# Sample attention in one round per half of the samples instead of one per key head

## The chip, the cores and the metric

The kernel runs on one core of one Trainium2 chip. The metric is the time of one execution on the device, in microseconds, as the median of several runs. The core has a matrix engine (TensorE, "PE" in the profile; its loads of the stationary operand are "PEld"), a vector engine (VectorE, "DVE"), an activation engine (ScalarE, "ACT"), a general engine (GpSimd, "POOL"), and queues that issue DMAs, here mostly that of SyncE ("SP"). Products land in PSUM banks of 128 partitions x 512 floats; everything else lives in SBUF.

## The reference, cut to what matters

One layer of a hybrid decoder runs for a prompt of 1024 tokens and for 8 sample sequences of 8 new tokens each: a SwiGLU block, a mixing block (sliding-window attention beside a gated linear recurrence, "hgrn"), and a second SwiGLU block, all float32. The change concerns the attention of the samples, which see a cache of 128 older keys and values:

```python
def cached_window_attention(q, k, v, sinks, k_buf, v_buf):
    kk = jnp.concatenate([k_buf, k], axis=1)          # 128 cached + 8 new keys
    vv = jnp.concatenate([v_buf, v], axis=1)
    s = jnp.einsum('bqhgd,bkhd->bhgqk', q, kk) * SCALE # 2 key heads x 4 query heads, 64 wide
    dist = (Wb + jnp.arange(Ld))[:, None] - jnp.arange(Wb + Ld)[None, :]
    mask = (dist >= 0) & (dist <= WINDOW)
    p = sink_probs(s, mask, sinks)                     # softmax with a learned sink per head
    out = jnp.einsum('bhgqk,bkhd->bqhgd', p, vv)
```

## The kernel before

**Groups.** The tokens are worked on in three groups n = 0, 1, 2: 256 prompt tokens with the 64 sample tokens (width 320), and twice 384 prompt tokens. Dense products (`mm3`, lines 242 to 244: three products of split operands in place of one float32 product) make up nearly all of TensorE's work. They use four PSUM banks with the tag `mm`. All the small products of attention, recurrence, norms and transposes share four banks with the tag `ax` (`axbank`).

**Side work by steps.** The small work is written as generators that stop at each `yield`. Between pieces of dense work the kernel calls `tick()`, which advances two queues, `at` (attention) and `hg` (recurrence), and the streams of norms (`c0`, `c1`, `c2`, `half`), each with its rate. A queue entry carries a declared number of steps; `pace` divides the steps left by the ticks left until the group is due:

```python
DUE = {0: 132, 1: 208, 2: 256}
for n, _, left in q:
    sofar += left
    rate = max(rate, sofar / max(1, DUE[n] - now[0]))
owed[k] += rate        # whole steps that are owed are taken at this tick
```

Ticks are counted from the start of `w_in_units(0)`. That makes 44 ticks (the attention's entries of group 0 join the queue after 12 of them, the recurrence's after 36), then come the rest of the first SwiGLU's down products (`f1.pair`, 48 ticks), then `w_in_units(1)` (44), and at tick 136 `need_mix(0)` takes whatever steps of group 0 are left before `w_out_units(0)` uses the result. A prompt block (`attn_block`, declared 9 steps) really has 11 stops: scores and softmax of half its heads, transposes, value products, the same for the other half, then scaling, gain (`finish_attn`, L1137), transposes (L1142) and the split copy `put_mix` (L1128, L1129). The recurrence's sample part (`sample_hgrn`) runs in the other queue at the same time; its products write the tiles `skT`, `sav` and `su`. Streams `c1` and `c2` form the input of groups 1 and 2 (`post_n`, then `pre_n` with transposes at L419 and split copies at L423 and L424). L220 is the vector half of splitting weights, L949 empties the banks of `f1.pair`.

**Order on an engine.** Each engine takes its instructions in the order in which a scheduler lays them out when the kernel is built, from simulated times; `issue_after(x)` only fixes that an instruction stands behind x on its engine. Buffers are slots behind a tag: `t2` has eight slots, which the sample attention shares with the norms and the recurrence.

**The sample attention** (`sample_attn`) handles the samples in two halves `hb` of four, and in each half the two key heads `g` one after the other. A round for one `hb` and one `g` has three steps: scores (L1383: four products, one per sample, each of 64 rows and 32 columns, rows 0 to 63 for g = 0 and 64 to 127 for g = 1, into the tile `ssc`) with the softmax on VectorE and ScalarE; transposes of the probabilities (L1400, L1401, tile `spT`) with two copies; value products with the cached values (L1408) and with the 8 new ones (L1412), tile `spv`, then scaling and a DMA to `osc`. A float32 product appears as two records in the trace. Four rounds make 12 steps; with the loads ahead and the gathering and `finish_attn` behind there are 17.

Of the kernel before, what the change touches and what calls it, by code (L numbers as in the profile page):

```python
# [18 lines left out]
P = 128  # L19
# [25 lines left out]
def tile_step(ctx: ExitStack, tc: tile.TileContext, A: dict, O: dict):  # L45
# [17 lines left out]
    def axbank(s="ax"):  # L63
        return ps.tile([P, 512], F32, tag="ax", bufs=4, name=uid(s))
# [948 lines left out]
    def mixing(tp, h):  # L1013
# [339 lines left out]
        def sample_attn():  # L1353
# [23 lines left out]
            osc = dr.tile([4, P, 64], F32, name="osc")  # L1377
            for hb in range(2):
                vc = cached("cache_v_win", hb)
                for g in range(2):  # L1380
                    bank = axbank("ssc")
                    for i in range(4):
                        PE.matmul(bank[32 * i:32 * i + 32, :136],  # L1383
                                  qs[64 * g:64 * g + 64, 4 * hb + i].rearrange("p m t -> p (m t)"),
                                  keys[64 * g:64 * g + 64, 4 * hb + i], start=True, stop=True)
# [12 lines left out]
                    yield  # L1398
                    bank = axbank("spT")
                    PE.transpose(bank[:, :P], p[:, :P], ident)  # L1400
                    PE.transpose(bank[:8, P:2 * P], p[:, P:136], ident)  # L1401
                    pT = t2((P, 2, P))
                    V.tensor_copy(pT[:, 0], bank[:, :P])
                    V.tensor_copy(pT[:8, 1], bank[:8, P:2 * P])
                    yield
                    ob = axbank("spv")
                    for i in range(4):
                        PE.matmul(ob[32 * i:32 * i + 32, :64], pT[:, 0, 32 * i:32 * i + 32],  # L1408
                                  vc[:, i, g * 64:g * 64 + 64], start=True, stop=False, skip_group_check=True)
                    for i in range(4):  # L1410
                        c = i * P + g * 64
                        PE.matmul(ob[32 * i:32 * i + 32, :64], pT[:8, 1, 32 * i:32 * i + 32],  # L1412
                                  vnb[hb][:8, c:c + 64], start=False, stop=True, skip_group_check=True)
# [362 lines left out]
```

## Time and profile before

| what | value |
|---|---|
| median of 3 runs | 1960.67 us (1960.13 to 1961.73) |
| the profiled execution, its own time | 1958.28 us |
| its span in the profile | 1956.2 us |
| TensorE busy | 1942.2 us, 99% |
| VectorE busy | 1368.3 us, 70% |
| ScalarE busy | 930.1 us, 48% |
| granted TensorE clock | 0.999 |
| first and last start of the sample scores (L1383) | 841.1 and 903.3 us |

The span is the stretch from the first to the last instruction in the profile. A view by lines gives for each group of instructions its engine, the shape, the count, the busy time and the mean of one. A timeline gives start, duration and the instruction, with neighbours of one kind merged ("x8"). Matmuls are pipelined, so their durations overlap; the distance between the starts of two dense products is what one of them costs.

### The profile page before, as it was taken

To read this page: it belongs to the slowest core of one execution; us is meant where nothing else is said; L and a number is where in the kernel's file an instruction comes from. 1 tells how busy PE (TensorE), PEld (TensorE's weight loads), DVE (VectorE), ACT (ScalarE), POOL (GpSimd) and SP (SyncE) were. 2 spreads that over 40 slices of the span, in tenths; PEclk is the share of its full clock that TensorE was granted. 3 is DMA by queue.
4 is the path that set the end of the run, shared out by engine and by line. 5 is a ranking of instruction groups with operands and counts; after the bars stand their busy time and mean duration, and the time that the engine had idled before them with its cause. 6 is when DMAs were issued, how large, how long until landed. Compare 5 with 4: busy or idle time off the path is not lost.

```text
span 1956.2 us, 34187 instructions
## 1 busy us (share of the span) xinstructions
PE 1942.2 (99%) x13469; PEld 1826.3 (93%) x13469; DVE 1368.3 (70%) x2210; ACT 930.1 (48%) x1628; POOL 208.1 (11%) x213
## 2 busy tenths in 40 slices
PE   9999999999999999999999999999999999999998
PEld 8999999999998988788899998999999999999887
DVE  7976667876557666876677676755987877655666
ACT  6533333444445544644345565655544444444453
POOL 0000000000004112111232224011000000000202
PEclk9999999999999999999999999999999999999999
DMA  7443345556667546765434344556555645667874
GB/s 267 147 145 145 149 163 176 176 189 212 237 227 229 178 130 182 233 200 148 125 115 150 97 126 120 167 160 207 165 206 191 218 171 187 210 237 234 305 260 141
DMA packets 160396, 358.20 MB, mean 183 GB/s; under 512 B 16284, under 2 KB 59996, under 8 KB 160220
## 3 DMA queue, kind: packets, MB, share of 16 engines
q1 hardware_dynamic: 159228, 354.19, 54.9%
q8 instruction: 105, 1.72, 0.4%
q10 hardware_dynamic: 1008, 1.84, 0.3%
q14 instruction: 55, 0.45, 0.1%
HBM read 279.33 MB, written 77.63 MB: 182 GB/s over the span
## 4 chain that ended last, share of the span: by engine, by line
PE 95%; DMA 2%; DVE 2%; ACT 1%; issue 0%; POOL 0%; SPq 0%; DVEq 0%; POOLq 0%; ACTq 0%
PE mm L242 28%; PE mm L244 28%; PE mm L243 28%; DMA ar<-fa 1%; PE c L244 1%; PE c L242 1%; PE c L243 1%; PE sc L1163 1%; PE pv L1204 1%; PE lv L1237 1%; PE pT L1189 1%; DVE w L220 0%; PE av L1338 0%; PE su L1460 0%; PE av L1341 0%
## 5 line engine op out<-in xcount | busy, mean ns | idle before, releaser
L242 PE MATMUL mm<-h,wsph 128*128 128x320 f32 (+1 forms) x1296 | 415.6, 321 | 2.6 <-DVE sg L668 2.6
L243 PE MATMUL mm<-h,wsph 128*128 128x320 f32 (+1 forms) x1296 | 410.0, 317 | 0.0
L244 PE MATMUL mm<-h,wspl 128*128 128x320 f32 (+1 forms) x1296 | 408.3, 316 | 0.1
L220 DVE TENSOR_TENSOR wspl<-raw,wsph 128x1024 fp32r<-128x1024 f32 x200 | 250.3, 1252 | 148.3 <-ACT wsph L219 143.0
L219 ACT CAST wsph<-raw 128x1024 fp32r<-128x1024 f32 x200 | 209.1, 1048 | 298.1 <-PE mm L243 246.6
L219 ACT CAST w<-raw 128x512 fp32r<-128x512 f32 (+1 forms) x226 | 169.5, 754 | 242.0 <-PE mm L243 116.7
L220 DVE TENSOR_TENSOR w<-raw,w 128x512 fp32r<-128x512 f32 (+1 forms) x226 | 196.6, 873 | 85.0 <-ACT w L219 84.7
L242 PEld LDWEIGHTS mm<-h,wsph 128*128 128x128 f32 x1296 | 243.3, 188 | 9.7 <-issue 4.5
L243 PEld LDWEIGHTS mm<-h,wsph 128*128 128x128 f32 x1296 | 243.5, 188 | 1.8 <-issue 0.8
L244 PEld LDWEIGHTS mm<-h,wspl 128*128 128x128 f32 x1296 | 243.0, 188 | 1.9 <-issue 1.0
L242 PE MATMUL mm<-h,w 128*128 128x384 f32 x704 | 235.6, 335 | 0.0
L243 PE MATMUL mm<-h,w 128*128 128x384 f32 x704 | 235.6, 335 | 0.0
L244 PE MATMUL mm<-h,w 128*128 128x384 f32 x704 | 230.5, 335 | 0.0
L242 PE MATMUL mm<-w,h 128*128 128x512 f32 x462 | 181.5, 396 | 1.3 <-DVE big L949 1.3
L243 PE MATMUL mm<-w,h 128*128 128x512 f32 x462 | 180.2, 390 | 0.0
L244 PE MATMUL mm<-w,h 128*128 128x512 f32 x462 | 178.9, 391 | 0.3 <-DVE h L220 0.3
L213 POOL TENSOR_TENSOR sm<-sm,mhalf 128x3 f32<-128x3 f32 (+4 forms) x37 | 35.4, 960 | 1188.8 <-DVE sm L297 522.4
L242 PEld LDWEIGHTS mm<-h,w 128*128 128x128 f32 x704 | 132.1, 188 | 0.2 <-ACT big L763 0.2
L243 PEld LDWEIGHTS mm<-h,w 128*128 128x128 f32 x704 | 132.1, 188 | 0.0
L244 PEld LDWEIGHTS mm<-h,w 128*128 128x128 f32 x704 | 131.7, 188 | 0.0
L219 ACT CAST w<-t 128x512 fp32r<-128x512 f32 x176 | 106.9, 621 | 49.3 <-PE mm L244 46.0
L220 DVE TENSOR_TENSOR w<-t,w 128x512 fp32r<-128x512 f32 x176 | 118.6, 685 | 11.9 <-ACT w L219 11.8
(340 smaller groups left out, 3685.8 us busy)
## 6 DMA issues: line engine op xcount, KB each, us to landing
raw<-in_ffn_w_gu_dram SPq DMA_DIRECT2D x154, 512.0 KB
raw<-in_ffn_w_down_dram SPq DMA_DIRECT2D x74, 512.0 KB
raw<-in_w_in_dram SPq DMA_DIRECT2D x54, 512.0 KB
ar<-fa SPq DMA_DIRECT2D x70, 384.0 KB
big<-in_ffn_w_down_dram SPq DMA_DIRECT2D x88, 256.0 KB
fb<-big SPq DMA_DIRECT2D x44, 512.0 KB
raw<-fb SPq DMA_DIRECT2D x40, 512.0 KB
fa<-big SPq DMA_DIRECT2D x22, 768.0 KB
```

The costliest lines, as they stand in the source:

```text
L213: G.tensor_tensor(y, x, mhalf[:y.shape[0], :y.shape[1]], op=ALU.pow)
L219: S.copy(hi, src)
L220: return (lo_eng or V).tensor_tensor(lo, src, hi.bitcast(F32), op=ALU.subtract)
L242: PE.matmul(out, a[0], b[0], start=first, stop=False, skip_group_check=resume)
L243: PE.matmul(out, a[0], b[1], start=False, stop=False, skip_group_check=resume)
L244: return PE.matmul(out, a[1], b[0], start=False, stop=last, skip_group_check=resume)
L1163: PE.matmul(banks[g][:, i * 256:i * 256 + wk], zq[64 * g:64 * g + 64, 2 * pr + i, b * P:(b + 1) * P], kx[64 * g:64 * g + 64, k0:k0 + wk], ...
L1189: PE.transpose(bank[:, (i * nk + kb) * P:(i * nk + kb + 1) * P], pt[g][:, i, kb * P:(kb + 1) * P], ident)
L1204: PE.matmul(ob[q0:q0 + 64, c:c + 64], pT[g][:, k1:k1 + 64], vn[:, vb, g * 64:g * 64 + 64], start=kb == 0, stop=kb == nk - 1)
L1237: PE.matmul(b4[ps_, j, a], x[:, a, cs], y[:, a, cs], start=True, stop=True)
```

## The change

Both key heads of a half go through one round. The scores of g = 1 and then of g = 0 are issued into two banks (the second four held behind the first by `issue_after`), then the softmax is made for both; both pairs of transposes go into one bank, which two longer copies empty; the value products of both go side by side into one bank, head 0's cached and new values and then head 1's; two scalings and two DMAs follow. The round has three steps instead of twice three, and the entry in the queue declares 11 steps instead of 17.

```diff
             for hb in range(2):
                 vc = cached("cache_v_win", hb)
+                banks = [axbank("ssc") for _ in range(2)]
+                for g in (1, 0):
+                    with tc.issue_after(last) if g == 0 else nullcontext():
+                        for i in range(4):
+                            last = PE.matmul(banks[g][32 * i:32 * i + 32, :136],
+                                             qs[64 * g:64 * g + 64, 4 * hb + i].rearrange("p m t -> p (m t)"),
+                                             keys[64 * g:64 * g + 64, 4 * hb + i], start=True, stop=True).ins
+                ps_, sms = [], []
                 for g in range(2):
-                    bank = axbank("ssc")
-                    for i in range(4):
-                        PE.matmul(bank[32 * i:32 * i + 32, :136],
...
                     p = t2((P, 136))
                     sm = small()
-                    V.tensor_tensor_reduce(out=p, in0=bank[:, :136], in1=smask, op0=ALU.add, op1=ALU.max,
+                    V.tensor_tensor_reduce(out=p, in0=banks[g][:, :136], in1=smask, op0=ALU.add, op1=ALU.max,
                                            scale=1.0, scalar=NEG, accum_out=sm[:, 0, 0:1])
...
-                    yield
-                    bank = axbank("spT")
-                    PE.transpose(bank[:, :P], p[:, :P], ident)
-                    PE.transpose(bank[:8, P:2 * P], p[:, P:136], ident)
-                    pT = t2((P, 2, P))
-                    V.tensor_copy(pT[:, 0], bank[:, :P])
-                    V.tensor_copy(pT[:8, 1], bank[:8, P:2 * P])
-                    yield
-                    ob = axbank("spv")
+                    ps_.append(p)
+                    sms.append(sm)
+                yield
+                bank = axbank("spT")
+                for g in range(2):
+                    PE.transpose(bank[:, 2 * g * P:(2 * g + 1) * P], ps_[g][:, :P], ident)
+                    PE.transpose(bank[:8, (2 * g + 1) * P:(2 * g + 2) * P], ps_[g][:, P:136], ident)
+                pT = t2((P, 2, 2, P))
+                bank = bank.rearrange("p (g j t) -> p g j t", g=2, j=2)
+                V.tensor_copy(pT[:, :, 0], bank[:, :, 0])
+                V.tensor_copy(pT[:8, :, 1], bank[:8, :, 1])
+                yield
+                ob = axbank("spv")
+                for g in range(2):
                     for i in range(4):
-                        PE.matmul(ob[32 * i:32 * i + 32, :64], pT[:, 0, 32 * i:32 * i + 32],
+                        PE.matmul(ob[32 * i:32 * i + 32, g * 64:g * 64 + 64], pT[:, g, 0, 32 * i:32 * i + 32],
                                   vc[:, i, g * 64:g * 64 + 64], start=True, stop=False, skip_group_check=True)
                     for i in range(4):
...
+                for g in range(2):
                     o = t2((P, 64))
-                    V.tensor_scalar(o, ob[:, :64], sm[:, 1, 2:3], None, op0=ALU.mult)
+                    V.tensor_scalar(o, ob[:, g * 64:g * 64 + 64], sms[g][:, 1, 2:3], None, op0=ALU.mult)
                     nc.sync.dma_start(osc[2 * g + hb], o)
-                    yield
+                yield
...
-                    gens += [(sample_attn(), 17), (kv_out(0), 1)]
+                    gens += [(sample_attn(), 11), (kv_out(0), 1)]
```

More of the change, by code (lines that the diff above doesn't have):

```diff
@@ L1379, in sample_attn @@
                 vc = cached("cache_v_win", hb)
-                for g in range(2):
-                    bank = axbank("ssc")
-                    for i in range(4):
-                        PE.matmul(bank[32 * i:32 * i + 32, :136],
-                                  qs[64 * g:64 * g + 64, 4 * hb + i].rearrange("p m t -> p (m t)"),
-                                  keys[64 * g:64 * g + 64, 4 * hb + i], start=True, stop=True)
+                banks = [axbank("ssc") for _ in range(2)]
[6 more added lines that the diff above has]
+                ps_, sms = [], []
+                for g in range(2):
                     p = t2((P, 136))
                     sm = small()
-                    V.tensor_tensor_reduce(out=p, in0=bank[:, :136], in1=smask, op0=ALU.add, op1=ALU.max,
+                    V.tensor_tensor_reduce(out=p, in0=banks[g][:, :136], in1=smask, op0=ALU.add, op1=ALU.max,
                                            scale=1.0, scalar=NEG, accum_out=sm[:, 0, 0:1])
@@ L1411, in sample_attn @@
                         c = i * P + g * 64
-                        PE.matmul(ob[32 * i:32 * i + 32, :64], pT[:8, 1, 32 * i:32 * i + 32],
+                        PE.matmul(ob[32 * i:32 * i + 32, g * 64:g * 64 + 64], pT[:8, g, 1, 32 * i:32 * i + 32],
                                   vnb[hb][:8, c:c + 64], start=False, stop=True, skip_group_check=True)
+                for g in range(2):
                     o = t2((P, 64))
-                    V.tensor_scalar(o, ob[:, :64], sm[:, 1, 2:3], None, op0=ALU.mult)
+                    V.tensor_scalar(o, ob[:, g * 64:g * 64 + 64], sms[g][:, 1, 2:3], None, op0=ALU.mult)
                     nc.sync.dma_start(osc[2 * g + hb], o)
-                    yield
+                yield
             o = t2()
```

## Prediction, made before the changed kernel was run

> **What bounds the kernel now.** I read the page first, then the busy time by stage, then the list of TensorE's waits, and then TensorE's timeline around each small group of the sample attention.
>
> ```profile
> span 1956.2 us, 34187 instructions
> PE 1942.2 (99%) x13469; PEld 1826.3 (93%) x13469; DVE 1368.3 (70%) x2210; ACT 930.1 (48%) x1628; POOL 208.1 (11%) x213
> PE 95%; DMA 2%; DVE 2%; ACT 1%; issue 0%; POOL 0%; SPq 0%; DVEq 0%; POOLq 0%; ACTq 0%
> ```
>
> TensorE is busy in 1942.2 of 1956.2 us and carries 95% of the chain that ended last. So a change is worth what it takes from TensorE's own stream, plus what it adds to or takes from the 14 us in which TensorE waits. By stage (columns: length, then the busy time of PE, PEld, DVE, ACT, POOL, then clock, DMA share, GB/s):
>
> ```profile
> 650.00:841.00 191.00, 187.71 (x1559) 160.62 (x1557) 129.23 (x213) 101.38 (x185) 31.95 (x35) 1.00 0.57 172
> 841.00:941.00 100.00, 100.00 (x651) 84.39 (x651) 69.77 (x122) 44.58 (x80) 21.49 (x21) 1.00 0.59 180
> 941.00:1300.00 359.00, 358.82 (x3739) 333.42 (x3739) 243.96 (x433) 195.91 (x391) 85.45 (x85) 1.00 0.43 129
> ```
>
> The second row is the stretch in which the sample attention runs. TensorE is busy in all of it, VectorE 70 us of 100, ScalarE 45. The clock is 1.00 throughout. Nothing there waits for the sample attention, so its latency is free; only the TensorE time of its groups counts. In the first row 3.3 us are idle, and the list of waits says for what:
>
> ```profile
> PE kT L1333 <- DVE h L424: 1.7, 1, 1.7
> PE mm L242 <- DVE big L949: 1.3, 2, 0.9
> PE mm L244 <- DVE h L220: 0.3, 1, 0.3
> ```
>
> These lie next to VectorE and to evictions, not in the sample attention.
>
> **The change part by part. Scores.** One group of before is 8 records (4 products, two records each) on a 64-row by 32-column piece of the array. Columns: start, duration, what.
>
> ```profile
> 840.55 0.39 PE L243 MATMUL mm<-w,h 128*128 128x512 f32 x1
> 840.78 0.39 PE L244 MATMUL mm<-w,h 128*128 128x512 f32 x1
> 841.10 0.44 PE L1383 MATMUL ssc<-big,t 64*32 64x136 f32 x8
> 841.46 0.50 PE L242 MATMUL mm<-w,h 128*128 128x512 f32 x1
> 841.80 0.39 PE L243 MATMUL mm<-w,h 128*128 128x512 f32 x1
> ...
> L1383 PE MATMUL ssc<-big,t x8: 275/288/302, 841.1 to 841.3; 64*32 64x136 f32 x8
> ```
>
> Dense 512-column products start 0.23 us apart (840.55 to 840.78). From 840.78 to 841.80 there should be 0.46 and there are 1.02 us, so the group costs 0.56. All eight records start within 0.2 us, so most of the price is going into the small shape and back. The change puts the four products of key head 1 (rows 64 to 127 of the array) and then the four of key head 0 (rows 0 to 63) in one group. What the second four add is bounded by the last group of before, which by chance has company from the other queue:
>
> ```profile
> 902.83 0.34 PE L244 MATMUL mm<-h,wspl 128*128 128x384 f32 x1
> 903.10 0.32 PE L1383 MATMUL ssc<-big,t 64*32 64x136 f32 x4
> 903.12 0.30 PE L1450 MATMUL sav<-big,big 64*32 64x128 f32 x2
> 903.47 0.44 PE L242 MATMUL mm<-h,wsph 128*128 128x384 f32 x1
> 903.75 0.34 PE L243 MATMUL mm<-h,wsph 128*128 128x384 f32 x1
> ```
>
> This `ssc` group is that of key head 1, on rows 64 to 127; the four L1450 records go through rows 0 to 63 with the same shape. Between 903.10 and 903.47 both kinds run mixed, in 0.37 us where the scores alone took 0.36 (841.10 to 841.46). So the second row half is nearly free: 0.01 for four records, 0.02 for eight. I take 0.05 for the second four products, as their columns overlap all four of the first (low end 0.02; high end 0.36, the group's own time once more, if the halves ran in line). A merged group costs 0.61 instead of 2 x 0.56 = 1.12.
>
> Not all four groups of before pay 0.56. From 902.83 to 903.75 are 0.92 us against 0.35 for two dense products, 0.57 for both kinds; the scores' own part lies between 0 and 0.57, and I take 0.28. Before pays 3 x 0.56 + 0.28 = 1.96, after 2 x 0.61 = 1.22: **0.74 less** (ends: 0.2 more, with the shared group at 0 and the halves in line; 1.1 less, with four full groups before and a free second half).
>
> **Transposes.**
>
> ```profile
> 866.99 0.33 PE L244 MATMUL mm<-h,wspl 128*128 128x384 f32 x1
> 867.16 0.34 PE L242 MATMUL mm<-h,wsph 128*128 128x384 f32 x1
> 867.34 0.27 PE L1400 MATMUL spT<-ident,t 128*128 128x128 f32 x1
> 867.47 0.42 PE L243 MATMUL mm<-h,wsph 128*128 128x384 f32 x1
> 867.73 0.34 PE L244 MATMUL mm<-h,wspl 128*128 128x384 f32 x1
> ...
> 966.06 0.31 PE L243 MATMUL mm<-h,wsph 128*128 128x320 f32 x1
> 966.21 0.31 PE L244 MATMUL mm<-h,wspl 128*128 128x320 f32 x1
> 966.36 1.03 PE L1189 MATMUL pT<-ident,t 128*128 128x128 f32 x8
> 967.38 0.31 PE L243 MATMUL mm<-h,wsph 128*128 128x320 f32 x1
> ```
>
> Two records cost 0.57 - 2 x 0.17 = 0.23, or 0.11 each. Eight of the prompt's in a row cost 967.38 - 966.21 - 2 x 0.15 = 0.87, again 0.11 each. There is no entry price, so joining two pairs **saves 0** (ends -0.05 and +0.05). VectorE makes four copies out of the bank per half of the samples before and two longer ones after; VectorE is not on the path here.
>
> **Value products.**
>
> ```profile
> 852.15 0.34 PE L242 MATMUL mm<-h,wsph 128*128 128x384 f32 x1
> 852.42 0.32 PE L1408 MATMUL spv<-kv,t 128*32 128x64 f32 x8
> 852.67 0.31 PE L1412 MATMUL spv<-vnew,t 8*32 8x64 f32 x8
> 852.91 0.44 PE L243 MATMUL mm<-h,wsph 128*128 128x384 f32 x1
> 853.19 0.34 PE L244 MATMUL mm<-h,wspl 128*128 128x384 f32 x1
> ```
>
> The group costs 1.04 - 0.35 = 0.69, of which 0.25 is the part with the cached values and 0.24 the part with the new ones. The change keeps the order cached, new, cached, new, so it still changes shape three times inside: 0.69 + 0.25 + 0.24 = 1.18 instead of 1.38. That is 0.20 per half of the samples, **0.40 less** (ends 0, and 1.4 if the second pair were free). The Trainium skill, "TensorEngine Tiling (Array Packing)", Key Properties, says that a change of the tiling mode drains the engine, so one can also count changes of shape: three in a group of 0.69, five in a merged one, an estimate of 1.15; a score group has two before and after, 0.56. By that count the sum below is 1.30 instead of 1.14; the trace agrees with it in that transposes, at full shape, have no entry price.
>
> **Queues and slots.** The stores to `osc` on SP's queue stay four; they now come in pairs after a group's two scalings, behind which weight loads stand that run ahead by two or three tiles. They cost nothing as long as those tiles last. Of the eight slots with the tag `t2` the sample attention holds four (two of new values, queries, cached values), then two probability tiles and the transposed one: seven instead of six.
>
> **Pacing.** The declared steps of the sample attention fall from 17 to 11. In group 0 the queue then has 30 instead of 36 steps between ticks 12 and 132, 0.25 instead of 0.30 a tick. Worked through tick by tick, the second prompt block finishes (scaling, gain, transposes) at ticks 89 to 95 instead of 77 to 83, and the sample scores come at ticks 103 and 111 instead of 90, 98, 105 and 113. The end of group 0 stays at tick 132, ahead of `need_mix(0)` at 136. This moves work past the one place where TensorE waits:
>
> ```profile
> 813.00:816.00 3.00, 2.38 (x10) 1.99 (x11) 3.00 (x4) 2.46 (x6) 2.35 (x2) 1.00 0.95 333
> 816.00:819.00 3.00, 1.33 (x8) 0.78 (x7) 3.00 (x5) 1.98 (x5) 2.86 (x2) 1.00 0.32 67
> ...
> L1171 DVE CUSTOM_DVE_ANT_0 t<-sc,amask 128x128 f32<-128x128 f32 (+1 forms) x16 | 4.8, 353 | 2.7 <-PE sc L1163 2.6
> L1192 DVE COPY t<-pT 128x256 f32<-128x256 f32 (+1 forms) x4 | 2.2, 545 | 0.0
> L1137 DVE SCALAR_TENSOR_TENSOR t<-t,sm,aon 128x512 f32<-128x512 f32 x2 | 1.5, 745 | 0.0
> L1214 DVE TENSOR_TENSOR t<-pv,sm 128x512 f32<-128x512 f32 x2 | 1.4, 688 | 0.2 <-PE pv L1204 0.2
> ```
>
> VectorE is full there (3.00 of 3.00) and TensorE works 2.38 and 1.33 of 3. L1214 and L1137 (0.69 + 0.75 = 1.4 us) leave that neighbourhood; four reductions (4 x 0.35 = 1.4 us) and a copy (0.55) of the block's second half move into it. I count the exchange as 0, with 2.9 us less (the waits of 1.7, 0.9 and 0.3 vanish, which lie in and beside these two rows) and 2 us more as ends.
>
> **The sum.** 0.74 + 0 + 0.40 + 0 = 1.14 us less. The profiled execution took 1958.28 us (span 1956.2 and 2.1 around it), 2.4 below the median of 1960.67. So 1957.1 for that execution, and 1959.5 as a median. That is 0.06%; a measurement of this kernel can tell about 0.2%, or 3.9 us, from no change.
>
> **The rivals.** *The waits go.* If the crowding in these rows dissolves because the block's finish leaves it, 2.9 us more go: 1956.6, just beyond the 0.2%. For it speaks that VectorE is the releaser of the 1.7 and 1.3 us; against it, that as much VectorE work moves in.
>
> *The banks run short.* Scores now hold two of the four `ax` banks at once. The state products of the other queue hold one throughout, so one is left for the 8 transposes by which group 2's input is formed (L419). Each transposed bank is freed by VectorE. The price of one late release is the 1.7 us of L1333 behind L424. It decides from three late releases on (5.1 - 1.1 = 4.0 us slower); with four it is 6.8 - 1.1, 1966.4. Against it: in the 100 us around the samples VectorE is free 30 us and TensorE never waits, and the prompt's scores already take two banks. The Trainium skill, "TensorEngine Tiling (Array Packing)", Restrictions and Gotchas, warns of just this: row tiling raises the pressure on PSUM, since row tiles write to different banks.
>
> *The halves run in line.* The change then does not do what it says: a score group costs 0.92, two of them 1.84, 0.12 less than 1.96 instead of 0.74, and the time is 1960.2, not to be told from no change.
>
> **How the numbers follow.** The sum as it stands, waits moving by up to 1.5 us either way: 0.71, with its own range 1957.5 to 1961.5. Halves in line: 0.05, also within 0.2%. The waits go: 0.13, faster. The banks: 0.11, slower. So faster 0.13, same 0.76, slower 0.11. The range takes in the case without waits and part of the banks' (two late releases, 1962.9): 1956.2 to 1963.2.
>
> **What would show it.** In the profile after: scores as x16 in one group at about 0.6 us between the dense products around it; value products as x8, x8, x8, x8, about 0.25 apart; transposes at 0.11 a record. TensorE busy in all of 841 to 941, waits of the same size between 800 and 830. I am wrong if a wait over 2 us stands beside L419 or a score group, or if the waits on L424 and L949 are gone.

## The result, and the profile after

| | before | after |
|---|---|---|
| median | 1960.82 us (1960.02 to 1962.06, 10 runs) | 1956.55 us (1954.40 to 1957.26, 10 runs) |
| ratio, 95% interval | | 0.9975 [0.9967, 0.9983] |
| profiled execution, span | 1958.28, 1956.2 us | 1956.50, 1954.6 us |

The change makes the kernel 4.3 us faster (3.3 to 6.5 by the interval). The forecast was 1.1 us, within what cannot be told from no change, with 0.76 on that side; what came is the rival *The waits go*, put at 1956.6 and 0.13. The page of after begins:

```profile
span 1954.6 us, 34186 instructions
PE 1943.6 (99%) x13469; PEld 1829.0 (94%) x13469; DVE 1362.4 (70%) x2206; ACT 929.5 (48%) x1627; POOL 215.2 (11%) x213
```

TensorE is busy 1.4 us more than in before and the span is 1.6 us shorter: idle time has gone. That TensorE is busy for longer comes from the start-up, in which the clocks of the two profiles differ; their rows from 27 to 31 us, before and then after (columns as in the row by stage below):

```profile
27.00:31.00 4.00, 4.00 (x30) 4.00 (x29) 3.79 (x8) 2.86 (x5) 0.00 (x0) 1.00 0.73 222
27.00:31.00 4.00, 4.00 (x18) 4.00 (x19) 3.79 (x8) 2.19 (x4) 0.04 (x1) 0.57 0.64 235
```

By the 3800th dense product, at about 650 us, after is 1.9 us late. From there to the last dense product it takes 1295.87 us and before 1299.34, so 3.5 us less, and that is the part that the change can touch. The busy time by stage of after (length, PE, PEld, DVE, ACT, POOL, clock, DMA share, GB/s) says where:

```profile
650.00:841.00 191.00, 190.57 (x1566) 162.55 (x1565) 130.41 (x212) 100.50 (x183) 33.59 (x36) 1.00 0.55 171
841.00:941.00 100.00, 100.00 (x668) 85.92 (x667) 68.65 (x121) 45.78 (x81) 23.03 (x20) 1.00 0.61 189
```

From 650 to 841 us TensorE is idle for 0.4 us where it was idle for 3.3; the 1.7 us on L424 and the 0.9 and 0.4 on L949 are no longer in after's list of waits, which has for this stretch:

```profile
PE pT L1189 <- DVE h L424: 0.2, 1, 0.2
PE mm L244 <- DVE h L220: 0.2, 1, 0.2
```

The groups of the sample attention themselves came out as worked out. TensorE's timeline of after, around a score group and a group of value products:

```profile
870.39 0.34 PE L244 MATMUL mm<-h,wspl 128*128 128x384 f32 x1
870.66 0.46 PE L1384 MATMUL ssc<-big,t 64*32 64x136 f32 x16
871.05 0.45 PE L242 MATMUL mm<-h,wsph 128*128 128x384 f32 x1
871.33 0.34 PE L243 MATMUL mm<-h,wsph 128*128 128x384 f32 x1
```

```profile
893.57 0.34 PE L243 MATMUL mm<-h,wsph 128*128 128x384 f32 x1
893.84 0.32 PE L1416 MATMUL spv<-kv,t 128*32 128x64 f32 x8
894.09 0.31 PE L1420 MATMUL spv<-vnew,t 8*32 8x64 f32 x8
894.34 0.32 PE L1416 MATMUL spv<-kv,t 128*32 128x64 f32 x8
894.59 0.31 PE L1420 MATMUL spv<-vnew,t 8*32 8x64 f32 x8
894.83 0.44 PE L244 MATMUL mm<-h,wspl 128*128 128x384 f32 x1
895.11 0.34 PE L242 MATMUL mm<-h,wsph 128*128 128x384 f32 x1
```

Two dense products at 0.17 are taken off: the scores cost 871.33 - 870.39 - 0.34 = 0.60 us (forecast 0.61), the value products 895.11 - 893.57 - 0.34 = 1.20 (forecast 1.18), stepping by 0.25.

One more profile of the unchanged kernel before bears on how its first profile is read. Its row of the stage and its largest waits there:

```profile
650.00:841.00 191.00, 187.01 (x1560) 160.37 (x1560) 128.57 (x213) 100.85 (x183) 32.00 (x35) 1.00 0.56 175
...
PE kT L1333 <- DVE h L424: 1.7, 1, 1.7
PE mm L242 <- DVE big L949: 1.2, 2, 0.8
```

The expectation was 1.7 and 0.9 us again and 3.3 us idle within 0.3, if the waits belong to the order of the work. The two waits came again (1.7, 0.8), but 4.0 us are idle instead of 3.3, in an execution of 1961.04 us. So a difference of 0.7 us between two profiles says nothing here. The profile the prediction was worked from was 2.4 us below its median; it reaches the 3800th dense product 2.0 us earlier than this second one, which has the slower stretch at 27 us as after has.

### The profile page after: what moved, and what is told of

It is laid out like the page before. It is cut to its first block, busy times and chain, and to the rows that moved or that the text cites. A ratio compares the mean times of both kernels' runs of the same rounds, so it can differ in the third digit from the quotient of the medians.

```text
span 1954.6 us, 34186 instructions
## 1 busy us (share of the span) xinstructions
PE 1943.6 (99%) x13469; PEld 1829.0 (94%) x13469; DVE 1362.4 (70%) x2206; ACT 929.5 (48%) x1627; POOL 215.2 (11%) x213
## 4 chain that ended last, share of the span: by engine, by line
PE 97%; DVE 1%; ACT 1%; DMA 0%; issue 0%; SPq 0%; DVEq 0%; POOLq 0%; POOL 0%; ACTq 0%
PE mm L242 29%; PE mm L244 29%; PE mm L243 29%; PE c L242 1%; PE c L244 1%; PE c L243 1%; PE sc L1163 1%; PE pv L1204 1%; PE lv L1237 1%; PE pT L1189 1%; PE av L1338 0%; PE u L1344 0%; PE l L1277 0%; PE av L1341 0%; DMA big<-in_x0T_dram 0%
## 5 line engine op out<-in xcount | busy, mean ns | idle before, releaser
L219 ACT CAST wsph<-raw 128x1024 fp32r<-128x1024 f32 x200 | 209.1, 1047 | 279.2 <-PE mm L243 223.1
L219 ACT CAST w<-raw 128x512 fp32r<-128x512 f32 (+1 forms) x226 | 169.6, 754 | 255.6 <-PE mm L243 127.9
L219 ACT CAST w<-t 128x512 fp32r<-128x512 f32 x176 | 106.9, 621 | 49.5 <-PE mm L244 45.8
```

Of the source, the lines that this page charges most:

```text
L219: S.copy(hi, src)
```

## The experiments

Two parts of the change can be had one without the other: the pacing (declared 11 instead of 17) and the merged groups. Then come the suspects for the waits. Line numbers shift by a few where lines were added. "Idle" is 191 us less TensorE's busy time from 650 to 841 us, with its parts ahead of and behind 800 us in brackets; "L391" are the starts of the first and the last of the six instructions of the norm of group 1 (`post_n` of `c1`) that add the residual.

| kernel | ratio [95%] | idle, us (ahead of 800, behind) | L391, us |
|---|---|---|---|
| before (first profile, second profile) | 1, 1.0002 [0.9992, 1.0011] | 3.3 (0.4, 2.9), 4.0 (1.1, 2.9) | 799.9-805.0, 802.6-807.7 |
| after | 0.9975 [0.9967, 0.9983] | 0.4 (0, 0.4) | 790.1-795.2 |
| e1 pace only | 1.005 [1.0038, 1.0062] | 0.4 (0, 0.4) | 791.4-796.4 |
| e4 declared 14 | one time, 1964.8 us | 1.0 (0, 1.0) | 791.3-796.2 |
| e6 pace only, handover held | 0.9968 [0.9956, 0.9981] | 0.4 (0, 0.4) | 790.4-795.5 |
| e2 merge only | 0.9993 [0.9984, 1.0001] | 3.9 (0.9, 3.0) | 802.2-807.3 |
| e7 merge only, handover held | 0.9993 [0.9985, 1.0002] | 3.8 (0.9, 2.8) | 802.1-807.3 |
| e3 values by kind, part left out | 0.9966 [0.9955, 0.9978] | 0.4 (0, 0.4) | 791.7-796.8 |
| e9 values by kind | 0.9965 [0.9952, 0.9977] | 0.4 (0, 0.4) | 790.7-795.7 |
| e8 no gain | 0.9993 [0.9983, 1.0002] | 4.0 (0.9, 3.0) | 801.0-806.1 |
| e11 no reductions | 1.0 [0.999, 1.0009] | 3.6 (1.3, 2.3) | 800.6-806.4 |
| e10 loads on ScalarE's queue, slots free | 1.0001 [0.9992, 1.0011] | 5.0 (1.3, 3.7) | 797.4-804.8 |
| e10 slots free | 1.0001 [0.9992, 1.0011] | 4.7 (1.4, 3.3) | 802.9-808.2 |
| e15 loads first | 0.9999 [0.9989, 1.0008] | 4.0 (2.0, 2.1) | 800.1-805.3 |
| e15 loads first, slots free | 0.9994 [0.9985, 1.0004] | 2.7 (1.0, 1.7) | 796.6-800.6 |
| e13 no loads | 0.9981 [0.9972, 0.9991] | 2.3 (1.6, 0.7) | 796.9-801.4 |
| e16 after, norm later | 1.0001 [0.9992, 1.0011] | 4.3 (0, 4.3) | 791.6-809.6 |
| e17 finish later | 1.0013 [1.0004, 1.0023] | 6.1 (1.6, 4.6) | 801.5-806.6 |
| e18 no second half | 0.9996 [0.9987, 1.0006] | 4.1 (2.7, 1.4) | 794.8-802.0 |

**Pacing or merging.** Each alone, by the declared number only:

```diff
-                    gens += [(sample_attn(), 17), (kv_out(0), 1)]     # e1: before
+                    gens += [(sample_attn(), 11), (kv_out(0), 1)]
-                    gens += [(sample_attn(), 11), (kv_out(0), 1)]     # e2: after
+                    gens += [(sample_attn(), 17), (kv_out(0), 1)]
```

> The kernel before with one number changed: the sample attention declares 11 steps, as the changed kernel does, but its rounds stay one per key head. Pacing theory (the change gained most of its time because the second prompt block is finished at ticks 89 to 95 instead of 77 to 83, away from the crowded stretch of VectorE at 810 to 822 us): TensorE's idle time in 650 to 841 us falls from 3.3 to about 0.4 us, the four score groups and value groups stay as before, and the time falls by about 2.9 us, to 1957.9 beside 1960.8 (ratio 0.9985). Rival, the merged rounds themselves brought it: idle time stays at 3.3 and the time at 1960.8.

> The changed kernel, but with 17 declared steps for the sample attention, so that the prompt blocks are paced as in the kernel before. Pacing theory: TensorE waits about 2.9 us beside L949 and L424 at 811 to 822 us as before, the merged groups cost 0.6, 0.44 and 1.19 us, and only their saving of 1.2 us is left: 1959.6 beside 1960.8 (ratio 0.9994). Rival, the merged rounds brought it: idle time 0.4 in 650 to 841 us and 1956.5 (0.9978).

> The kernel before with 14 declared steps: by the pacing rule the second prompt block then makes its scaling and gain at tick 83 and its transposes at 88, between the two kernels (77 and 83 before, 89 and 95 after). Pacing theory: these steps are already past tick 80, at which the three banks of a down product are emptied, so TensorE's idle time in 650 to 841 us is under 1.5 us instead of 3.3. Rival (the waits depend on the merged rounds): 3.3.

e2 did what the pacing theory said: waits as before, some 1.4 us gained. e1 lost its idle time in the stage as its theory said, but the kernel became 11 us slower instead of 2.9 us faster. The longest of its waits that before does not have:

```profile
PE oT L1142 <- DVE t L1137: 6.3, 1, 6.3
...
PE u L1344 <- DVE sm L1171: 2.4, 1, 2.4
```

The sample attention of before really has 17 steps. By the rule of `pace`, with 11 declared they crowd at ticks 129 to 133 and push the first block of group 1 from tick 134 to 136, and everything behind is laid out anew; e4, with 14 declared, shows the same (1.0 us idle in the stage, 3.0 us on L1344 later). So the number declared has two effects, and they had to be parted. In e6 and e7 the entry is corrected at the first step of the sample attention, so that the blocks ahead of it keep the pace wanted and the handover to group 1 (its first block's first step) stays at tick 134 or near it:

```diff
+            queues["at"][0][2] += 6      # e6: before, declared 11;  e7: after, declared 17, -6
```

> The kernel before (one round per key head) with 11 declared steps, and 6 more added to the entry at the sample attention's first step. So the prompt blocks are paced as in the changed kernel, the sample attention runs its 17 steps at ticks 101 to 130, and group 1's blocks start at tick 134 as before. Pacing theory, with the hand-over to group 1 as the reason why 11 declared steps alone lost 11 us: TensorE's idle time in 650 to 841 us is 0.4, no wait over 2 us stands beside L1142 or L1344, and the time is 2.9 us under before: 1958.0 beside 1961.0 (0.9985). Rival, the old rounds do not fit into the shorter stretch: it stays above 1965 as with 11 alone.

> The changed kernel with 17 declared steps, and 6 taken off at the sample attention's first step, so that the prompt blocks are paced as in the kernel before and group 1's blocks start at tick 132 instead of 125. Pacing theory: the waits at 811 to 822 us are those of before (3.3 us idle in 650 to 841), the merged groups save their 1.2 us and nothing is lost later: 1959.8 beside 1961.0 (0.9994). Rival, the merged rounds bring the whole gain when nothing is lost later: 1956.6.

The row of the stage of e6, whose waits there are the two of 0.2 us that after has, and the largest waits of e7:

```profile
650.00:841.00 191.00, 190.58 (x1562) 162.27 (x1561) 129.63 (x211) 101.28 (x184) 33.34 (x36) 1.00 0.55 173
```

```profile
PE kT L1333 <- DVE h L424: 1.7, 1, 1.7
PE mm L242 <- DVE big L949: 1.5, 3, 0.7
```

The pacing alone gives 0.9968, the whole gain, with the sample attention as it was; the merging alone 0.9993, twice, about 1.4 us and at the edge of what can be told. The two do not add up: by the medians after (1956.55 us) is not below e6 (1956.15), and from the 3800th dense product to the last e6 takes 1296.4 us, 0.5 more than after, where the sum had 1.14 for the merging. One reason is in e6's timeline of TensorE: with the pacing moved, most of the unmerged score groups and groups of value products share a gap with each other or with the recurrence's.

```profile
912.49 0.34 PE L242 MATMUL mm<-h,wsph 128*128 128x384 f32 x1
912.76 0.32 PE L1409 MATMUL spv<-kv,t 128*32 128x64 f32 x8
913.01 0.31 PE L1413 MATMUL spv<-vnew,t 8*32 8x64 f32 x8
913.25 0.44 PE L1384 MATMUL ssc<-big,t 64*32 64x136 f32 x8
913.62 0.44 PE L243 MATMUL mm<-h,wsph 128*128 128x384 f32 x1
913.90 0.34 PE L244 MATMUL mm<-h,wspl 128*128 128x384 f32 x1
```

Value products and scores in one gap cost 913.90 - 912.49 - 0.34 = 1.07 us, not 0.69 + 0.56 = 1.25.

**The value products by kind.** Both cached sets first, then both new ones:

```diff
                 for g in range(2):
                     for i in range(4):
                         PE.matmul(ob[...], pT[:, g, 0, ...], vc[:, i, g * 64:g * 64 + 64],
-                                  start=True, stop=False, skip_group_check=True)
+                                  start=g == 0, stop=False, skip_group_check=True)   # e9; e3 keeps start=True
+                for g in range(2):
                     for i in range(4):
```

> The changed kernel with the value products of a round in another order: the cached values of both key heads, then the new values of both. Theory that the price is the change of shape (128 rows for cached, 8 for new values): three changes instead of five, a value group falls from 1.19 to about 0.75 us, twice, so 0.9 us less than the changed kernel: 1955.7 beside 1960.8 (0.9974). Rival, each set of eight records costs its 0.25 us wherever it stands: 1.19 us and 1956.5.

> The changed kernel with the value products by kind (cached values of both key heads, then new values of both), only the first key head's cached products with the start flag. In the kernel that had the flag on both the group cost 0.92 us, against 1.19 in the changed kernel. Theory, a kind costs 0.25 us for its first eight records and 0.14 for its second: again 0.92, 0.54 us less for the two rounds, 1956.0 beside 1961.0 (0.9975, the changed kernel 0.9977). Rival, the flag has a price of its own: a group of 1.19.

In e3 the second start flag drops the cached part of head 0, so that this part is left out there. TensorE's timeline of e9:

```profile
893.61 0.34 PE L243 MATMUL mm<-h,wsph 128*128 128x384 f32 x1
893.88 0.43 PE L1416 MATMUL spv<-kv,t 128*32 128x64 f32 x16
894.24 0.43 PE L1421 MATMUL spv<-vnew,t 8*32 8x64 f32 x16
894.60 0.44 PE L244 MATMUL mm<-h,wspl 128*128 128x384 f32 x1
894.87 0.34 PE L242 MATMUL mm<-h,wsph 128*128 128x384 f32 x1
```

A group costs 894.87 - 893.61 - 0.34 = 0.92 us instead of 1.20: eight more records of a kind cost 0.11, against 0.25 behind a change of kind. The same 0.92 stands in e3, between the 0.75 of its theory and the 1.19 of its rival; changes of shape are not the whole price, as this group has three of them like the group of before, which costs 0.69. Twice 0.28 us is 0.03%, which the times (0.9965 beside 0.9975) do not resolve; by its median and ratio e9, at 1955.83 us, is the fastest kernel here.

**Why the waits go: amounts of VectorE work.** The prediction's rival laid the waits to block 1's finish beside them; I had set against it that as much work moves in. e8 leaves out the gain L1137 in that block, e11 the four reductions of its second half:

```diff
-            V.scalar_tensor_tensor(o[:r], o[:r], sm[:r, 1, 0:1], aon[:r], ...)           # e8
+            if gain: V.scalar_tensor_tensor(o[:r], o[:r], sm[:r, 1, 0:1], aon[:r], ...)
-                        V.tensor_tensor_reduce(out=p[:, i, :wk], in0=banks[g][...], in1=mask, ...)   # e11
+                        if not left_out: V.tensor_tensor_reduce(...)
```

> The kernel before without the VectorE instruction L1137 (the multiplication by the norm's gain) in group 0's second prompt block, so that this block's output lacks its norm; it took 0.75 us of VectorE at 810 us, ahead of the evictions L949. Crowding theory (VectorE's total work at 810 to 822 us makes TensorE wait): the waits on L949 and L424, 2.6 us together, fall by about 0.75 each, so the time falls by 1 to 1.5 us: 1959.7. Rival, the waits come from the order of the banks and not from the amount of VectorE's work: both waits stay within 0.2 us and the time at 1961.0.

> The kernel before, pacing as before, without the four reductions (L1171, 4 x 0.35 = 1.4 us of VectorE) of the second half of prompt block 1: the exponentials read the score banks directly with the first half's maxima, so the mask and the own maxima of that half are left out. Theory (VectorE's queue at 784 to 786.5 delays the additions of the down product, hence the weight splits, the weight loads that wait for them on SyncE's queue, the six loads of the residual tiles behind these, and by that the whole norm of the next layer): the additions at 786.32 come some 1.4 us earlier, the residual tiles are there by about 798 instead of 803.5, TensorE's waits on L424 and L949 shrink from 2.6 us to at most 1.3, idle from 650 to 841 us from 3.3 to at most 2, time 1.3 to 2.6 us below before. Rival 1 (the order of the loads on SyncE's queue and their slots, not VectorE's amount of work, keeps the residual tiles late): idle stays at 3.0 to 3.6, time within 1 us of before. Rival 2 (the norm's work collides with the prompt block's finish whatever the loads do): idle stays at 3 or above although the residual tiles come 2 us earlier.

Both left the idle time where it was (4.0, 3.6), and L424 still makes TensorE wait 1.7 us in both. In e8 the waits on L949 did not fall either (1.9 us); its time, 0.9993, cannot be told from no change, nor from the 1 to 1.5 us of its crowding theory. e11 is less clean, as the edit brings a wait of its own, on the exponentials that now read the score banks:

```profile
PE pT L1191 <- ACT t L1182: 1.3, 1, 1.3
PE mm L242 <- DVE big L949: 0.4, 1, 0.4
```

So 0.75 or 1.4 us less work on VectorE did not shorten the stage, but e11 does not show that it could not.

**The residual loads.** Between before and after one thing differs plainly on SyncE's queue. Its timeline in before, then in after:

```profile
789.43 6.05 SPq L924 DMA_DIRECT2D raw<-fb  x2
795.57 2.79 SPq L389 DMA_DIRECT2D xt<-in_x_prompt_dram  x6
```

```profile
782.47 2.33 SPq L389 DMA_DIRECT2D xt<-in_x_prompt_dram  x5
784.89 0.66 SPq L924 DMA_DIRECT2D raw<-fb  x1
789.36 0.33 SPq L389 DMA_DIRECT2D xt<-in_x_prompt_dram  x1
```

In before the six loads of residual tiles stand behind two weight loads that hold the queue for 6.05 us, and are issued 13 us later. The six additions that use them, by line, in before and in after (count, ns min/median/max, first and last start):

```profile
L391 DVE SCALAR_TENSOR_TENSOR big<-big,sm,xt x6: 745/746/753, 799.9 to 805.0; 128x512 f32<-128x512 f32 x6
...
  DMA xt<-in_x_prompt_dram: 3.6, 1
```

```profile
L391 DVE SCALAR_TENSOR_TENSOR big<-big,sm,xt x6: 742/744/747, 790.1 to 795.2; 128x512 f32<-128x512 f32 x6
```

VectorE stands 3.6 us for them in before, and the rest of the norm follows some 4 us later than in after (the first L411 at 808.2 instead of 804.5 us, the first L424 at 817.6 instead of 813.7), although after is 1.9 us late at the start of the stage. Five kernels act on this:

```diff
-                nc.sync.dma_start(xt, ...)                                           # e10 on ScalarE's queue
+                (nc.scalar if n == 1 and eps == 4 * EPS else nc.sync).dma_start(xt, ...)
-                    p = t2((P, 2, 256))                                              # slots free
+                    p = (tp.tile([P, 2, 256], F32, tag="vn" if g else "kx", ...)
+                         if (n, b) == (0, 1) else t2((P, 2, 256)))
-                    t = t2()
+                    t = m2() if (n, b, g) == (0, 1, 1) else t2()
+                    with tc.issue_after(xlast[0]) if xlast and n == 2 else nullcontext():   # e15: weight loads
+                        nc.sync.dma_start(raw[:, :n], FB[...])                               #   behind xlast
+                if n == 1 and eps == 4 * EPS: xt = t                                 # e13: no load
```

> The kernel before, pacing as before, loads on SyncE's queue as before; only the prompt block's probability tiles and one transposed tile lie in other buffers, so that the loads of the residual tiles wait for no slot. Theory A (they wait behind the two weight loads on the same queue, not for the slots): L391 begins where it does in before, 799.9 within 0.7 us, idle from 650 to 841 us 2.8 to 3.6, time within 1 us of before. Theory B (the slots hold them): L391 begins 3 us or more earlier, idle at most 1.5, time 1.8 to 3 us below before.

> The kernel before, pacing as before; the residual tiles of the chunk concerned are loaded from ScalarE's queue instead of SyncE's, and the prompt block's probability tiles and one transposed tile lie in other buffers, so that the loads wait for no slot. Theory (the late residual tiles are the cause: L391 waits 3.6 us for them and all that follows comes late): L391 waits under 0.5 us and begins at about 796 or earlier instead of 799.9, L949 and L424 release TensorE with less than 1 us in all instead of 2.6, idle from 650 to 841 us at most 1.5 instead of 3.3, time 1.8 to 3 us below before. Rival (the norm's place against the prompt block's finish decides, and the loads are only late company): L391 earlier, but idle between 2.5 and 3.6 and the time within 1 us of before.

> The kernel before, pacing as before; only the order on SyncE's queue is changed: the two weight loads that stood ahead of the six residual loads (L389) are held behind them, as they stand in the changed kernel. Theory (the residual tiles come late because their loads stand behind two weight loads, and the late norm that follows runs into the additions L949): L391 begins at 793 or earlier instead of 800 to 802.6, L411 begins 3 us or more earlier than 808 to 811, TensorE's waits on L424 and L949 fall from 2.6 us to at most 0.8, idle from 650 to 841 us from 3.3 to 4.0 to at most 1.5, time 2 to 4 us below before. Rival 1 (the place of the prompt block's finish decides, the loads are company): L391 earlier, idle still 2.8 or more, time within 1 us of before. Rival 2 (the weight loads pay): the two weight loads come later and TensorE waits for weight splits instead, 1 us or more on L219 or L220.

> As e15_xt_first, and the prompt block's probability tiles and one transposed tile lie in other buffers, so that the residual loads wait for no slot. Theory: as e15_xt_first; L391 at the same time or up to 3 us earlier, and no other difference in TensorE's waits, as they are gone already. If slots matter as well: idle from 650 to 841 us smaller than in e15_xt_first by over 0.7 us. Rival 1: idle 2.8 or more as there.

> The kernel before, pacing as before, without the six residual loads of this chunk: L391 adds the tile to itself instead of the residual, so that this part of the computation is left out and VectorE's instructions stay. Theory: L391 waits for no DMA and begins some 3 to 7 us earlier than 800 to 802.6, L424 and L949 release TensorE with at most 0.8 us in all, idle from 650 to 841 us at most 1.5, time 2 to 4 us below before. Rival 1 (the prompt block's finish): idle 2.8 or more, time within 1 us of before.

None of the five brought the idle time under 2 us. With the slots free and nothing else the loads stay behind the weight loads (L391 at 802.9, as in the second profile of before, 802.6; theory A), so slots alone are not the reason. On ScalarE's queue the last load was issued late and took long; the chain of that kernel has

```profile
797.38 7.38 DMA xt<-in_x_prompt_dram
```

and its last L391 starts at 804.8. Put first on SyncE's queue, the loads hold it for 9.7 us in e15, as they wait for their slots, and TensorE then waits for weight splits (rival 2). Its largest waits:

```profile
PE mm L242 <- ACT w L219: 1.5, 1, 1.5
PE mm L244 <- DVE h L220: 1.2, 1, 1.2
```

With the loads first and slots free, and with no loads at all, L391 ends its row at 800.6 and 801.4, and idle falls to 2.7 and 2.3 us: better than before's 4.0, far from after's 0.4. Where it falls tells more. The rows from 800 us on, first of e13, then of before:

```profile
800.00:841.00 41.00, 40.30 (x238) 33.55 (x238) 33.10 (x53) 26.74 (x63) 9.91 (x7) 1.00 0.69 208
800.00:841.00 41.00, 38.14 (x196) 31.04 (x194) 35.37 (x56) 26.15 (x55) 8.64 (x7) 1.00 0.71 231
```

Behind 800 us, where the late norm can act, e13 is idle for 0.7 us instead of 2.9 and the waits on L424 are gone. Most of what is left, 1.4 us, stands at 789 and 790 us, ahead of the additions, so late additions cannot be its cause. The time of e13, 0.9981, is 3.7 us below before and so most of what after gains. But its profile is of an execution of 1961.00 us, 3.2 us above its median, and has a new wait of 0.9 us at 881 us, so it does not show where the median gains. The time of e15 with slots free, 0.9994, cannot be told from no change.

**The other direction.** e16 is the changed kernel with that norm held back by two of its steps:

```diff
     def post_n(n, y, sm, xsrc, xdst, eps=4 * EPS):
+        if n == 1 and eps == 4 * EPS:
+            yield
+            yield
```

> The changed kernel; the norm that holds the residual loads starts two of its steps later, so that four of the six loads stand behind three weight loads on SyncE's queue. Pacing and merged groups as in the changed kernel, the prompt block's finish still at ticks 89 to 95. Theory: the last L391 at 801 or later instead of 795.2, waits of TensorE on L424, L949 or L411's successors come back with 1.5 us or more, idle from 650 to 841 us from 0.4 to at least 2, time 1.5 to 4 us above the changed kernel's ratio (0.998 to 1.0 of before). Rival 1 (the prompt block's finish decides): idle at most 1, time as the changed kernel, 0.9967 to 0.9978 of before.

Its largest wait in the stage, the load that its chain goes through ahead of it, and its row just behind that wait:

```profile
PE mm L242 <- ACT h L219: 3.3, 1, 3.3
...
822.79 5.89 DMA ar<-fa
...
830.00:833.40 3.40, 3.40 (x10) 2.63 (x9) 3.40 (x6) 2.15 (x5) 0.00 (x0) 0.50 0.40 114
```

4.3 us idle again, and the time is that of before: the whole gain is gone with the pacing of the block untouched. The largest wait has another name than in before: TensorE waits for a split of ScalarE (L219), and that for a load of activations, `ar`, which was issued at 822.8 us. In after this load is issued at 822.1 us, and the dense product that needs it starts at 828.7 us without a wait, only 0.9 us earlier than in e16 (829.6). The time ahead of it is filled there with 24 records of the recurrence's products (L1338, L1341, L1344, from 826.0 us); in e16 they come behind it, from 835.4 us. So holding the norm back is enough to lose the gain, but not by the waits of before: another wait is no longer covered by side work. Behind this wait the granted clock is 0.50 for 3.4 us and dense products start 0.43 us apart instead of 0.23; the idle column leaves out these 1.7 us (e17 has such a stretch from 823.7 us). No run here shows what sets it off.

**Which part of block 1.** The pacing moves its second half (reductions L1171 from 784 to 803 us) and its finish (L1137 from 810 to 833 us). One at a time:

```diff
+            for _ in range(6 if (n, b) == (0, 1) else 1):    # e17: ahead of the scaling
+                yield
+                left_out = (n, b, pr) == (0, 1, 1)           # e18: no reductions, exponentials and copies there;
+                if left_out:                                 #   the value products read the first half's
+                    for x in (sm[:, 0], sm[:, 1], mx[:, 1]):
+                        V.tensor_copy(of(x, 1), of(x, 0))
```

> The kernel before with five empty steps between the value products and the scaling of block 1 of group 0: its finish (scaling, gain, transposes, put_mix) comes at ticks 90 to 96 as in the changed kernel, its second half stays at ticks 66 to 74, group 1's first block still starts at tick 134. If the finish beside the norm is what makes TensorE wait (as the prediction's rival had it): idle from 650 to 841 us at most 1.2 instead of 3.3 to 4.0, time 2 to 3.5 us below before. If the second half is: L391 still begins at 799 or later, idle 2.5 or more, time within 1 us of before.

> The kernel before, pacing as before; of the second half of block 1 of group 0 VectorE's reductions, ScalarE's exponentials and the copies of the transposed probabilities are left out (the value products read the first half's), all products and transposes stay on TensorE, and the finish stays at ticks 77 to 85. If the second half (its vector and scalar work and its slots ahead of the norm) is what delays the norm: L391 begins at 793 or earlier, L411 at 806 or earlier, idle from 650 to 841 us at most 1.2, time 2 to 3.5 us below before. If the finish is: idle 2.5 or more, time within 1 us of before.

The largest wait in this stage of e17, then the two largest of e18:

```profile
PE kT L1334 <- DVE h L424: 3.6, 1, 3.6
```

```profile
PE mm L242 <- DVE big L949: 2.7, 2, 2.4
PE mm L242 <- ACT h L219: 1.4, 1, 1.4
```

Moving the finish alone made it worse (6.1 us idle, 1.0013), which refutes the reason that the rival gave. Taking away the second half's vector and scalar work alone left 4.1 us: L391 then begins at 794.8 but ends its row at 802.0. Of these 4.1 us, 2.7 stand ahead of 800 us (the 2.4 on L949 end at 788 us) and 1.4 behind, where before has 2.9. With the finish late in both, moving the rest of block 1 and the end of block 0 as well (e17 to e6) takes idle from 6.1 to 0.4.

So the idle time of before stands at two places, and over all profiles they follow different things.

- *Behind 800 us* (2.9 us in before) it follows the norm. Where the last of the six additions starts by 796.8 us, 0.4 to 1.0 us are idle there (after, e1, e3, e4, e6, e9); where it starts from 800.6 to 802.0, 0.7 to 1.7 (e13, e15 with slots free, e18); where it starts at 804.8 or later, 2.1 to 4.6. This is shown from both directions: with the pacing as before, three edits that brought the additions forward shortened the idle time, and in e16 holding the norm back brought it.
- *Ahead of 800 us* (0.4 and 1.1 us in before) it follows the pacing: every kernel paced as before has 0.4 to 2.7 us there, every kernel paced as after (e16 too) and e4 none. Which of the moved pieces does it no run here shows.

What makes the norm late in before is only partly resolved: the late loads and the second half of block 1 each carry a part, the finish does not, and each edit of before laid the instructions of several engines out anew, so that another wait often took the place of the one removed. Nor is it that the second half stands ahead of the additions on VectorE: in e4 its reductions do (788.9 to 790.3 us, the additions from 791.3), and idle is 1.0. No kernel here has the norm done by 796 us with block 1 as in before, so whether that alone would be enough stays open.

## Why the prediction was wrong, point by point

- *Scores, transposes, value products.* The prices of the merged groups are right: 0.61 and 1.18 are 0.60 and 1.20. What before pays is less sure than "3 x 0.56 + 0.28" has it: only the score group at 841.1 us stands alone in its gap. The one at 859.2 shares it with three records of transposes (0.84 us for both), and the third, at 879.2, stands among 26 records of other kinds between two dense products. Merging by itself gave 1.4 us by e2 and e7, where the sum had 1.14, but with intervals that reach to none. TensorE is busy in all of 841 to 941 us, as forecast. The estimate by changes of shape, 1.15 for the merged value products, came out a little low; the rule behind it (the Trainium skill, "TensorEngine Tiling (Array Packing)", Key Properties: a change of the tiling mode drains the engine) agrees with e9's trace in so far as two changes of shape fewer save 0.28 us there.
- *Queues and slots.* "They cost nothing as long as those tiles last" was said of the `osc` stores, and no wait stands at them. But the reading of SyncE's queue ended there. What counted on it was which loads stand ahead of which after everything has moved, 45 us (before) to 88 us (after) ahead of the first sample scores.
- *Pacing: the step that failed.* "I count the exchange as 0, with 2.9 us less ... and 2 us more as ends." The measured value is the low end and more: 2.9 us less idle time against the first profile, 3.6 against the second. The moved ticks were told rightly (the gain now comes at 833 us). Wrong was the measure: VectorE's microseconds that leave and enter the stretch. e8 and e11 took 0.75 and 1.4 us of them away and left the idle time as it was. What the runs showed in its place: the new pacing alone takes idle from 3.3 or 4.0 us to 0.4 (e6), most of it behind 800 us, where the waits follow the norm of group 1; that norm's additions wait 3.6 us for late residual loads in before and start 10 us earlier in after. Delaying the norm by two steps loses the whole gain (e16). The rest went ahead of 800 us, where no run here shows what does it.
- *The rival The waits go.* Its 2.9 us are the right waits. Its time, 1956.6, is the result to 0.1 us, which is in part luck: it adds 1.14 us of merging to the 2.9, and on top of the pacing the merging shows only 0.5 us in the profiles and nothing in the medians. Its reason, the block's finish, is refuted by e17. The argument that I held against it (as much work moves in) was true and beside the point.
- *The banks run short, The halves run in line.* No wait at L419 or at a score group in after (e7 has two at L419, of 0.5 and 0.4 us, far from three of 1.7); sixteen score records cost 0.60. Both are out.

## What to carry to other kernels

A declared step count is a schedule: before counting a moved block by its busy time, list what in-order queues (SyncE's loads first) stand behind it where it leaves and where it arrives, and give the wait that it leaves a real chance to vanish. When a change has a pacing side and a work side, run each alone and hold the handover to the next phase, or the one will be hidden by an accident of the other (e1 against e6). And once a single wait has been removed and another of the same size appears, as in e15, test the stretch as a whole from both directions instead of chasing the next name, and split it where the suspected step stands: idle time ahead of that step is not its doing.

## What the runs showed of the hardware that I had not expected

Small products of unlike kind that happen to share one gap in the dense stream cost less than two gaps (1.07 against 1.25 us in e6), so merging by hand and good neighbours compete for the same saving. Within a gap, eight further records cost 0.02 to 0.04 us on the other row half (0.60 in after against 0.56 in before and 0.58 for the one score group that stands alone in e6), 0.11 of the same kind on the same rows (e9), and 0.25 behind a change of kind (after).
